# A mixture-of-experts stage: one-hot columns and places made an expert ahead, gathers and scatters at other experts

## The chip, the cores and the metric

The kernel runs on one core of a Trainium2 chip. The metric is device time in microseconds of one execution. TensorE multiplies matrices into PSUM banks, VectorE and ScalarE work on PSUM and SBUF, GpSimd on SBUF, and SyncE issues all transfers from HBM.

## The reference

Two layers over 256 latent tokens and 256 context tokens of width 1024. Each layer has four token mixers and then an expert-choice mixture of 16 experts, in which each expert takes the 32 tokens (CAP) with the highest affinity to it. In the last layer only the latent tokens go through the experts.

```python
def expert_choice_ffn(u, p):
    cap = max(1, EC_CAPACITY * n // N_EXPERTS)                  # 2 * 256 / 16 = 32
    aff = jax.nn.softmax((u @ p['w_router']).astype(jnp.float32), axis=-1)
    gate, idx = lax.top_k(jnp.swapaxes(aff, 1, 2), cap)
    xe = jax.vmap(lambda ub, ib: ub[ib])(u, idx)                # tokens of each expert
    hg, hu = jnp.split(jnp.einsum('becd,edf->becf', xe, p['w_exp_in']), 2, axis=-1)
    ye = jnp.einsum('becf,efd->becd', jax.nn.silu(hg) * hu, p['w_exp_out']) * gate[..., None].astype(u.dtype)
    return jax.vmap(lambda yb, ib: jnp.zeros((n, d), yb.dtype).at[ib.reshape(-1)].add(yb.reshape(-1, d)))(ye, idx)
```

## The kernel before

**Streams.** Layer 0 has two streams (context and latent tokens, ns = 2), the last layer one (ns = 1). An expert's 32 tokens of each stream stand side by side, so its products load 64 columns of tokens in layer 0 and 32 in layer 1, and the expert's weights stream past them.

**Order.** The program is written by generators, one for each part of the work. A planner (class Order) keeps modelled clocks of the engines, and each `yield` tells it a cost or a time to wait for; from that it fixes the order of the instructions at build time. On the chip each engine runs its own instructions in that order and waits on semaphores.

**Loads.** loader() writes the loads of each expert's weights: 8 of `w_ei` (rows of the first product) and 4 of `w_eo` (the second), 1 MB each, in the order first(1), second(0), first(2), second(1), and so on. A load goes into one of NB = 12 large buffers (L1701, L1707; the last expert's second weights L1704), or in four parts into tiles of the small pool t2 (L1699; NT2 = 40 tiles, which nearly all other short-lived tiles share). A load's buffer is free when TensorE has read it. The weights of layer 1's mixers (L888) come through the same queue and the same large buffers.

**Experts.** experts() runs over x = 0 to 15. first(x) (L1956, products L1964) makes the gate and up products; ScalarE and VectorE turn them into `a` (L1975 to L1977). second(x - 1) (L1980, products L1989) is written behind it, so that it covers the making of `a`; VectorE multiplies its rows by the modulation into `ye` (L2001, four instructions of 32x512 in layer 0). Then TensorE transposes `a` (L2026).

**Gathers.** Four experts (a group, eg = x // 4) are gathered at once by gather(eg) (L1827): VectorE spreads the chosen token numbers into `im` (L1831), TensorE broadcasts them over the partitions (L1837), VectorE compares them with each partition's number and scales them, which gives the one-hot columns `hot` (L1842), TensorE multiplies the tokens `h` by them (L1853), and ScalarE and VectorE write the result, modulated, to `xe` (L1860, L1862). Group 0 is gathered in choose(), at the end of the routing; groups 1, 2 and 3 behind the first product of experts 3, 4 and 5.

**Scatters.** columns() (L1814) makes, once, the table of token numbers and gates by column, behind the gather at expert 5. places(eg, s) (L1868, L1871) makes from it the one-hot places `ot` of a group for a stream; scatter() (L1874) multiplies `ye` by them (L1879) and VectorE adds the result to `h` (L1881). The groups 0, 1 and 2 are scattered at experts 6, 10 and 14, behind that expert's second(x - 1); group 3 in last_expert() (L1896, products L1924, scatter L1912, additions L1887), half by half, and behind it the next layer's norms and transposes begin. filters(1), layer 1's convolution filters, runs between the experts from expert 9 on.

Of the kernel before, what the change touches and what calls it, by code (L numbers as in the profile page):

```python
# [27 lines left out]
CAP = 32  # L28
# [185 lines left out]
def _a(n):  # L214
    return 0.19 + n / 1200


def _d(n):
    return 0.07 + n / 960
# [7 lines left out]
def kernel(ctx: ExitStack, tc: tile.TileContext, x, ctxt, cols, skip, lamb, fng, ta, tb, tcn, td,  # L227
# [169 lines left out]
    def layer(l):  # L397
        last = l == DEPTH - 1
        streams = (1,) if last else (0, 1)
        ns = len(streams)  # L400
# [1376 lines left out]
        def choose():  # L1777
# [23 lines left out]
            for r in range(CAP // 8):  # L1801
# [6 lines left out]
                e = yield {"pe": 0.3 if r == 0 else 0.0, "dve": 1.4}  # L1808
            nc.vector.tensor_copy(idxf, idxu)
            top["i"], top["v"] = idxf, vals  # L1810
            yield from gather(0)
            x_ev[1].t = S.t["pe"]

# [12 lines left out]

        def gather(eg):  # L1827

            n = 4 * CAP
# [9 lines left out]
            for i, s in enumerate(streams):  # L1839
                for b in range(2):  # L1840
                    t = 2 * s + b
                    nc.vector.tensor_scalar(hot[:, 2 * i + b], p[:, i * n:(i + 1) * n], iotac[:, b:b + 1],  # L1842
                                            r_tok[t], op0=OP.is_equal, op1=OP.mult)
            e = yield {"pe": 0.43, "dve": 2 * ns * _d(n)}
            yield e
            xe[eg] = [t2("xe", w=8 * M).rearrange("p (k e c) -> p k e c", k=2, e=4) for _ in range(KC // 2)]
# [102 lines left out]
        def experts():  # L1949


            yield rt_ev
            ye, eaT, pend = {}, {}, None
            mod5 = mods[l]["r5"][0]
# [25 lines left out]
            def second(x):  # L1980
# [22 lines left out]
                yield {"dve": _d(512) * 2 * ns}  # L2003

            for x in range(NE):
                a = yield from first(x)
                act = yield {"act": _a(FW), "dve": 2 * _d(FW)}
                if x == F1:
                    f_ev.t = act
                if x in (3, 4, 5):  # L2010
                    yield from gather(x - 2)
                if x == 5:
                    yield from columns()
                if x:
                    yield from second(x - 1)
                    if x % 4 == 0:
                        pend = x // 4 - 1
                if pend is not None and x % 4 >= 2:
                    y = ye.pop(pend)
                    for s in reversed(streams):  # L2020
                        yield from scatter(s, y[s], places(pend, s))
                    y = pend = None
                yield act
# [115 lines left out]
```

## Time and profile before

| | us |
|---|---|
| median of 3 runs | 2040.72 (2034.96 to 2045.57) |
| the profiled execution, its own time | 2040.19 |
| its span in the trace | 2038.3 |
| TensorE busy | 1706.0 (84%) |
| VectorE busy | 972.9 (48%) |
| ScalarE busy | 573.0 (28%) |
| layer 0's expert stage, about | 692 to 1190 |
| layer 1's expert stage, about | 1580 to 2020 |

The busy shares are means over stages that differ: in the mixers most of the work is on weights that are split on the chip, in the expert stages 192 loads of 1 MB pass in each layer. A busy TensorE is not TensorE at its peak, since its instructions overlap. The granted clock (PEclk) is given as a share of 2.4 GHz; 0.5 is 1.2 GHz.

### The profile page before, as it was taken

How to read it: one execution, taken by the hardware profiler on the slowest of the kernel's cores; microseconds unless marked ns; L12 is line 12 of the kernel's file. 1: busy time of each engine (PE TensorE's matmuls, PEld its weight loads, DVE VectorE, ACT ScalarE, POOL GpSimd, SP SyncE). 2: the span in 40 equal slices, each digit the busy share in tenths (PEclk: the TensorE clock that was granted, in tenths of full speed). 3: DMA queues.
4: the chain of work that ended last, by engine and by line, in shares of the span. 5: the costliest groups of instructions: out<-in, count | busy, mean ns of one | idle time of the engine just before them, and what ended most of it. 6: DMA issues, size and time to landing. Idle time of an engine off the chain costs nothing.

```text
span 2038.3 us, 28201 instructions
## 1 busy us (share of the span) xinstructions
PE 1706.0 (84%) x11128; PEld 1108.9 (54%) x11128; DVE 972.9 (48%) x1690; ACT 573.0 (28%) x1301; POOL 502.6 (25%) x413
## 2 busy tenths in 40 slices
PE   5878887899999899899799888988998877666655
PEld 2657565776789734533233268877997443222222
DVE  4788898966644412221232267778765111101012
ACT  4434555544432100100100054456552000000001
POOL 1466788612101100000000023786321000000000
PEclk9999898999999899999999999999998976767778
DMA  7535335232236699989999954555579999999997
GB/s 275 191 109 186 122 130 171 88 99 59 71 104 227 227 368 414 373 348 417 415 414 418 409 168 150 167 170 186 157 234 354 403 411 412 415 413 412 414 412 292
DMA packets 204973, 550.75 MB, mean 270 GB/s; under 512 B 14054, under 2 KB 94120, under 8 KB 174760
## 3 DMA queue, kind: packets, MB, share of 16 engines
q1 hardware_dynamic: 204840, 548.94, 71.5%
q8 instruction: 88, 1.44, 0.3%
q14 instruction: 45, 0.37, 0.1%
HBM read 547.83 MB, written 1.05 MB: 269 GB/s over the span
## 4 chain that ended last, share of the span: by engine, by line
PE 45%; DMA 28%; DVE 16%; ACT 5%; issue 3%; POOL 3%; SPq 0%; ACTq 0%; DVEq 0%; POOLq 0%
DMA we<-in_w_ei_dram 12%; PE pm L1964 9%; DMA we<-in_w_eo_dram 9%; PE pm L355 6%; PE pm L357 6%; PE pm L356 6%; PE psc L1989 5%; DVE wq L349 3%; DMA h<-in_w_ei_dram 3%; PE psc L1853 2%; ACT wq L348 2%; PE psc L1879 1%; DVE aj L526 1%; DMA wi<-in_w_in_dram 1%; DVE ca L1246 1%
## 5 line engine op out<-in xcount | busy, mean ns | idle before, releaser
L1964 PE MATMUL pm<-we,xe 128*32 128x256 f32 (+1 forms) x2848 | 383.2, 523 | 86.7 <-DMA we<-in_w_ei_dram 84.6
L355 PE MATMUL pm<-uh,wq 128*128 128x256 f32 (+1 forms) x832 | 293.1, 352 | 16.4 <-ACT tg L1001 8.0
L1964 PEld LDWEIGHTS pm<-we,xe 128*32 128x32 f32 (+1 forms) x2848 | 131.1, 132 | 315.4 <-issue 161.1
L356 PE MATMUL pm<-ul,wq 128*128 128x256 f32 (+1 forms) x832 | 284.0, 341 | 2.9 <-DVE ul L785 1.6
L357 PE MATMUL pm<-uh,wq 128*128 128x256 f32 (+1 forms) x832 | 283.4, 341 | 0.0
L349 DVE TENSOR_TENSOR wq<-wi,wq 128x1024 fp32r<-128x1024 f32 x131 | 181.7, 1398 | 112.5 <-ACT wq L348 112.3
L1989 PE MATMUL psc<-we,eaT 128*32 128x256 f32 (+1 forms) x1344 | 185.7, 530 | 46.4 <-DMA we<-in_w_eo_dram 45.0
L1976 DVE SCALAR_TENSOR_TENSOR ea<-ea,pm 128x512 f32<-128x512 f32 (+1 forms) x32 | 17.7, 555 | 392.2 <-ACT ea L1975 392.2
L528 POOL TENSOR_TENSOR aw<-aw,cb 128x512 f32<-128x512 f32 x124 | 193.1, 1571 | 14.9 <-DMA aw<-in_ada_t_dram 9.0
L355 PEld LDWEIGHTS pm<-uh,wq 128*128 128x128 f32 x832 | 162.3, 195 | 40.4 <-ACT tg L1001 8.9
L356 PEld LDWEIGHTS pm<-ul,wq 128*128 128x128 f32 x832 | 162.0, 195 | 21.8 <-issue 4.1
L357 PEld LDWEIGHTS pm<-uh,wq 128*128 128x128 f32 x832 | 161.5, 194 | 16.9
L2001 DVE TENSOR_TENSOR ye<-psc,modr 32x512 f32<-32x512 f32 (+1 forms) x120 | 66.4, 554 | 212.9 <-PE psc L1989 211.6
L1989 PEld LDWEIGHTS psc<-we,eaT 128*32 128x32 f32 (+1 forms) x1344 | 63.2, 134 | 161.9 <-issue 91.7
L348 ACT CAST wq<-wi 128x1024 fp32r<-128x1024 f32 x132 | 136.2, 1044 | 15.1 <-DMA wi<-in_w_in_dram 13.0
L1975 ACT ACTIVATE ea<-pm 128x512 f32<-128x512 f32 (+1 forms) x32 | 15.7, 490 | 425.3 <-PE pm L1964 396.2
L1246 DVE SCALAR_TENSOR_TENSOR ca<-up,colt,ca 128x510 f32<-128x510 f32 (+29 forms) x120 | 116.7, 973 | 2.3
L1893 POOL TENSOR_TENSOR hg<-h,gr 128x512 f32<-128x512 f32 x2 | 2.6, 1294 | 463.3 <-ACT px L360 459.4
L2028 ACT COPY eaT<-pt 128x512 f32<-128x512 f32 (+1 forms) x32 | 15.3, 479 | 319.2 <-PE pt L2026 319.2
L528 POOL TENSOR_TENSOR ao<-aw,cb 128x512 f32<-128x512 f32 x60 | 98.4, 1640 | 20.3 <-DMA aw<-in_ada_t_dram 17.7
L1292 ACT ACTIVATE e<-psc,nm 128x512 f32<-128x512 f32 (+1 forms) x72 | 44.3, 616 | 144.4 <-DVE nm L1290 144.0
L660 POOL MEMSET hf<- 1x256 f32 x4 | 1.5, 376 | 318.3 <-ACT ab L656 318.3
(408 smaller groups left out, 3002.4 us busy)
## 6 DMA issues: line engine op xcount, KB each, us to landing
we<-in_w_ei_dram SPq DMA_DIRECT2D x230, 1024.0 KB, 12.7
we<-in_w_eo_dram SPq DMA_DIRECT2D x113, 1024.0 KB, 14.6
wi<-in_w_in_dram SPq DMA_DIRECT2D x58, 1024.0 KB, 5.5
aw<-in_ada_t_dram SPq DMA_DIRECT2D x160, 256.0 KB, 5.6
h<-in_w_ei_dram SPq DMA_DIRECT2D x56, 256.0 KB, 14.5
we<-in_w_ei_dram SPq DMA_DIRECT2D x48, 256.0 KB, 7.4
wbr<-in_w_branch_dram SPq DMA_DIRECT2D x40, 256.0 KB, 5.3
we<-in_w_eo_dram SPq DMA_DIRECT2D x36, 256.0 KB, 5.9
```

What stands on the lines that cost most here:

```text
L348: nc.scalar.copy(hi, src)
L349: eng.tensor_tensor(lo, src, hi.bitcast(F32), op=OP.subtract)
L355: nc.tensor.matmul(out, lh, rh, start=first and i == 0, stop=False)
L356: nc.tensor.matmul(out, lh, rl, start=False, stop=False)
L357: nc.tensor.matmul(out, ll, rh, start=False, stop=last and i == n - 1)
L528: nc.gpsimd.tensor_tensor(o, wt_, cb[s, k], op=OP.mult)
L1246: nc.vector.scalar_tensor_tensor(o, up[:, :, max(d, 0):256 + min(d, 0)], cw[:, c0 + d:c0 + d + 1], o, op0=OP.mult, op1=OP.add)
L1292: nc.scalar.activation(e, p[:, :nk], AF.Exp, scale=scale, bias=nm, accum_out=s)
L1853: nc.tensor.matmul(p[:, kk * n:(kk + 1) * n], h[2 * s + b][k // 4][:, (k % 4) * 128:(k % 4 + 1) * 128], hot[:, 2 * i + b], start=b == 0, s ...
L1964: nc.tensor.matmul(dst[j * M:(j + 1) * M, :], lhs, w[o + j * FW // 512][:, j * FW % 512:j * FW % 512 + FW], start=k == 0, stop=k == KC - 1 ...
L1989: nc.tensor.matmul(py[j * M:(j + 1) * M, :FW], aT[:, c * 128 + q * M:c * 128 + (q + 1) * M], w[f % 2 * 2 + j * FW // 512][:, j * FW % 512: ...
L2001: nc.vector.tensor_tensor(ye[eg][s][c0 // 512][e4 * CAP:(e4 + 1) * CAP, c0 % 512:c0 % 512 + FW], py[r0:r0 + CAP, :FW], mod5[r0:r0 + CAP, c ...
```

## The change

gather() is cut in two: taken(eg) makes `im`, the broadcast and `hot`, and gather(eg) makes the products. For groups 1 to 3, taken() is written ahead of the first product of the expert behind whose first product gather() stands; group 0 keeps its order. The gathers are written at experts 3, 5 and 7 in place of 3, 4 and 5, the table of columns ahead of the first product of expert 6. The places are made behind the second product of experts 7, 9 and 12, and the scatters stand at experts 8, 10 and 13, between the first product of that expert and the second product of the one ahead, in place of 6, 10 and 14 behind the second product.

```diff
--- before.py
+++ after.py
@@ -1808,6 +1808,7 @@
                 e = yield {"pe": 0.3 if r == 0 else 0.0, "dve": 1.4}
             nc.vector.tensor_copy(idxf, idxu)
             top["i"], top["v"] = idxf, vals
+            yield from taken(0)
             yield from gather(0)
             x_ev[1].t = S.t["pe"]
 
@@ -1824,7 +1825,9 @@
                 nc.vector.tensor_scalar(ic[:, 8 * j:8 * j + 4 * ns], p[:, 8 * j:8 * j + 4 * ns], 0.5 if j else 1.0, None, op0=OP.mult)
             yield {"pe": 0.3, "dve": 0.6}
 
-        def gather(eg):
+        hots = {}
+
+        def taken(eg):
 
             n = 4 * CAP
             im = t2("im", w=ns * n)[:R]
@@ -1841,8 +1844,14 @@
                     t = 2 * s + b
                     nc.vector.tensor_scalar(hot[:, 2 * i + b], p[:, i * n:(i + 1) * n], iotac[:, b:b + 1],
                                             r_tok[t], op0=OP.is_equal, op1=OP.mult)
+            hots[eg] = hot
             e = yield {"pe": 0.43, "dve": 2 * ns * _d(n)}
-            yield e
+            if eg == 0:
+                yield e
+
+        def gather(eg):
+
+            n, hot = 4 * CAP, hots.pop(eg)
             xe[eg] = [t2("xe", w=8 * M).rearrange("p (k e c) -> p k e c", k=2, e=4) for _ in range(KC // 2)]
             for k4 in range(2):
                 for i, s in enumerate(streams):
@@ -1950,7 +1959,7 @@
 
 
             yield rt_ev
-            ye, eaT, pend = {}, {}, None
+            ye, eaT = {}, {}
             mod5 = mods[l]["r5"][0]
 
             def first(x):
@@ -2002,24 +2011,29 @@
                                                 py[r0:r0 + CAP, :FW], mod5[r0:r0 + CAP, c0:c0 + FW], op=OP.mult)
                 yield {"dve": _d(512) * 2 * ns}
 
+            ots, ready = {}, {3: 1, 5: 2, 7: 3}
             for x in range(NE):
+                if x in ready:
+                    yield from taken(ready[x])
+                if x == 6:
+                    yield from columns()
                 a = yield from first(x)
                 act = yield {"act": _a(FW), "dve": 2 * _d(FW)}
                 if x == F1:
                     f_ev.t = act
-                if x in (3, 4, 5):
-                    yield from gather(x - 2)
-                if x == 5:
-                    yield from columns()
+                if x in ready:
+                    yield from gather(ready[x])
+                if x in (8, 10, 13):
+                    pend = (8, 10, 13).index(x)
+                    y = ye.pop(pend)
+                    for s in reversed(streams):
+                        yield from scatter(s, y[s], ots.pop(s))
+                    y = None
                 if x:
                     yield from second(x - 1)
-                    if x % 4 == 0:
-                        pend = x // 4 - 1
-                if pend is not None and x % 4 >= 2:
-                    y = ye.pop(pend)
-                    for s in reversed(streams):
-                        yield from scatter(s, y[s], places(pend, s))
-                    y = pend = None
+                if x in (7, 9, 12):
+                    ots.update({s: places((7, 9, 12).index(x), s) for s in reversed(streams)})
+                    yield {"dve": ns * _d(256)}
                 yield act
                 p = pt()
                 for c in range(FW // 128):
```

## Rows read from the trace of the kernel before

**Rows 1.** The page: the span.

```profile
span 2038.3 us, 28201 instructions
```

**Rows 2.** Windows: length, busy time (count) by engine, PEclk, DMA share, GB/s.

```profile
692.00:1190.00 498.00, 446.18 (x2036) 177.68 (x2037) 130.62 (x258) 43.58 (x87) 7.60 (x11) 0.95 0.98 391
1200.00:1575.00 375.00, 336.05 (x2566) 310.72 (x2566) 274.29 (x460) 196.48 (x446) 179.23 (x154) 0.96 0.60 196
1580.00:2020.00 440.00, 303.91 (x3250) 133.77 (x3242) 56.59 (x135) 18.10 (x48) 0.00 (x0) 0.76 1.02 411
```

**Rows 3.** Windows inside layer 0's expert stage, same columns.

```profile
820.00:920.00 100.00, 89.88 (x430) 42.87 (x432) 27.37 (x57) 8.97 (x21) 0.00 (x0) 0.93 0.90 359
920.00:1170.00 250.00, 226.53 (x960) 76.84 (x958) 62.51 (x103) 17.27 (x28) 6.54 (x9) 0.97 1.02 415
860.00:870.00 10.00, 8.26 (x55) 6.24 (x55) 2.15 (x9) 3.01 (x8) 0.00 (x0) 0.84 0.40 167
900.00:910.00 10.00, 8.16 (x15) 3.35 (x16) 5.09 (x9) 0.00 (x0) 0.00 (x0) 0.83 1.01 410
```

**Rows 4.** Waits of SyncE's queue, 840 to 880: total us, times, longest.

```profile
SPq L1707 <- PE psc L1989: 21.3, 4, 17.5
```

**Rows 5.** Last expert's second weights, their source line; SyncE's timeline behind.

```profile
L1704 SPq DMA_DIRECT2D we<-in_w_eo_dram x4: 368/1813/4080, 1151.8 to 1159.4; - x4
DMA to landing us min/median/max: 14.4/14.9/15.9
...
1162.13 14.85 SPq L888 DMA_DIRECT2D wi<-in_w_in_dram  x4
```

**Rows 6.** Waits of TensorE, 740 to 1190: total us, times, longest.

```profile
PE psc L1879 <- DVE ot L1871: 13.4, 6, 3.4
PE pm L1964 <- DMA we<-in_w_ei_dram: 6.4, 9, 2.3
PE psc L1837 <- DVE im L1831: 5.2, 3, 1.8
PE psc L1989 <- DMA we<-in_w_eo_dram: 4.9, 8, 0.7
PE psc L1821 <- DVE vm L1819: 1.7, 1, 1.7
```

**Rows 7.** TensorE's timeline: start, length, instruction, [idle before it, releaser].

```profile
750.73 13.95 PE L1964 MATMUL pm<-we,xe 128*64 128x512 f32 x64
772.07 13.96 PE L1964 MATMUL pm<-we,xe 128*64 128x512 f32 x64
787.70 0.69 PE L1837 MATMUL psc<-im,ones 32*128 32x256 f32 x2 [1.68 <-DVE im L1831]
788.90 9.02 PE L1853 MATMUL psc<-hot,h 128*128 128x128 f32 x64 [0.51 <-DVE hot L1842]
839.02 13.95 PE L1964 MATMUL pm<-we,xe 128*64 128x512 f32 x64
```

**Rows 8.** VectorE's timeline around expert 3, same columns.

```profile
771.60 2.78 DVE L2001 TENSOR_TENSOR ye<-psc,modr 32x512 f32<-32x512 f32 x4 [5.62 <-PE psc L1989]
787.24 0.41 DVE L1831 TENSOR_TENSOR im<-idxf,tat 32x256 f32<-32x256 f32 x1
```

**Rows 9.** TensorE's timeline: first and last scatter of layer 0.

```profile
900.74 5.40 PE L1879 MATMUL psc<-ye,ot 128*128 128x512 f32 x8 [3.33 <-DVE ot L1871]
907.24 3.70 PE L1879 MATMUL psc<-ye,ot 128*128 128x512 f32 x8 [1.10 <-DVE ot L1871]
1138.10 6.56 PE L1879 MATMUL psc<-ye,ot 128*128 128x512 f32 x8 [3.32 <-DVE ot L1871]
```

**Rows 10.** TensorE's timeline: layer 0's last products, layer 1's first.

```profile
1171.95 3.67 PE L1924 MATMUL pm<-we,eaT 128*64 128x256 f32 x32 [0.72 <-ACT eaT L2028]
1178.51 3.67 PE L1924 MATMUL pm<-we,eaT 128*64 128x256 f32 x32
1192.80 0.35 PE L355 MATMUL pm<-uh,wq 128*128 128x256 f32 x1 [0.24 <-DVE uh L846]
```

## The prediction, made before the changed kernel had run

> **What bounds the kernel now.** I read the views from coarse to fine. First the span [rows 1] and the busy time of the stretches [rows 2]: layer 0's expert stage (692 to 1190 us) runs its transfers at a share of 0.98 of the DMA engines, layer 1's mixers (1200 to 1575) at 0.60, layer 1's expert stage (1580 to 2020) at 1.02. TensorE is busy for 446 of 498 us in the first and only 304 of 440 us in the last. So layer 1's experts are bound by weight transfers alone, and the moves there (gathers and scatters of one stream, half the columns) fall into time in which TensorE waits for weights anyway. The question is layer 0.
>
> There the stretches tell more [rows 3]. From 920 to 1170 us the transfers run at 415 GB/s with a share of 1.02: full. From 820 to 920 us they give 359 GB/s at a share of 0.90, and from 860 to 870 us only 167 GB/s at 0.40. In that hole nothing is left in the queue, because the queue of SyncE waits for TensorE to read a buffer free: one wait of 17.5 us for the second product (L1989) [rows 4]. The last transfers of the stage are issued up to 1159.4 us and land 14.4 to 15.9 us later [rows 5], at about 1174.5 us; TensorE comes to the last product only at 1178.51 and ends it at 1182.2 [rows 10]. So the stage is bound by transfers, with one hole in the middle, and with TensorE some 8 us late at the end.
>
> The hole's cause: an expert needs 12 loads of 1 MB (1.049 million bytes), at 415 GB/s 30.3 us of transfer, 2.53 a load. TensorE needs 21.3 us for an expert without extras (first products start at 750.73 and 772.07) [rows 7]. A gather adds 1.68 us of waiting, 0.69 for the broadcast product, 0.51 of waiting and 9.02 for the gather itself [rows 7], 11.9 us: 33.2 us, slower than the transfers. Experts 3, 4 and 5 have one each and expert 6 a scatter, so four in a row are slower than 30.3 us; the 12 large buffers (NB) fill with weights that TensorE has not reached, and the queue stops.
>
> **The change part by part, layer 0.** No instruction is added or taken away, no transfer is moved; im, the broadcast product and hot (L1831 to L1842), the column table (L1814) and the places (L1871) move on VectorE and TensorE, whole gathers and scatters move between experts.
>
> *Gathers at 3, 5, 7.* Experts now cost TensorE alternately about 33 and 21 to 25 us (expert 6 has the column table): at most 58 per pair against 60.6 us of transfer. Buffers are read faster than filled from expert 3 on. At expert 5 the first product now ends at 853.0 us (839.02 + 13.95 [rows 7]) and the queue runs dry about 11 us later (share 0.40 of the ten from 860 [rows 3]): it held 11 us of transfers. With the gather of expert 4 gone (11.9) and the broadcast in front of expert 3's and 5's first products (some 3.4 us of it at expert 5) this product ends at about 844.8, 8 us earlier; of the transfers some 2.5 us more have run, since the small hole ahead of 853 is gone too. The queue then holds 11 + 8 - 2.5, about 16 us, and the longest stretch without a release is the gather and the first load of the second product, 11 us. It does not run dry. The hole is worth 100 x (1 - 0.90/1.02) = 11.8 us by share and 100 x (1 - 359/415) = 13.5 us by bytes [rows 3]. I take 12.5 us off the end of the transfers; lower bound 10, if 2 us or so reappear at expert 3, where the broadcast now holds back the first release, upper bound 13.5.
>
> *im ahead of the first product.* What is queued behind the broadcast product is the whole first product. VectorE does im right behind the four products of the previous expert's rows, which begin as the second product ends and take 2.78 us [rows 8]; with im itself at 0.41 [rows 8] TensorE waits 3.2 us less the 0.5 in which it still transposes (771.60 to 772.07 [rows 7, 8]), about 2.7 us, in place of 1.68 + 0.51 = 2.2 us. The columns at expert 6 wait in the same way, 2.7 us in place of 1.7 [rows 6]. Together four waits of 2.7, 10.8 us, for 5.2 + 1.7 [rows 6] and three times 0.51 [rows 7], 8.4 us, now: 2.4 us worse on TensorE. That costs nothing on the end as long as TensorE is not the later one (sum below).
>
> *Scatters between a first and a second product.* Now the places and the rows' product stand between the second product and the scatter: waits of 13.4 us in six [rows 6], 3.33 + 1.10 in a pair [rows 9]. After the long wait the scatter's first half takes 5.40 and 6.56 us where the second half takes 3.70 [rows 9], and the granted clock of 900 to 910 us is 0.83 [rows 3], so part of it ran at 1.2 of 2.4 GHz: 1.7 and 2.9 us, with the third estimated like the smaller one 6.3 us. In the new place the expert's rows and the places are a whole expert old; the wait is nothing (upper bound: 1.10 each, if VectorE's additions hold back TensorE's banks). TensorE gains 13.4 + 6.3 = 19.7 us.
>
> *Where the gain goes.* From the first product at 772.07 to the last expert's at 1171.95 [rows 7, 10] TensorE now takes 399.9 us. Less 11.3 of waits for weights [rows 6], 19.7 of the scatters, plus 2.4: 370.9 us, so it could be at the last expert at 1143. The last expert's first load lands three loads (3 x 2.53 us) ahead of the last one: 1174.5 - 12.5 - 7.6 = 1154.4 us. So transfers set the end, with 11 us of slack on TensorE, and what the scatters save beyond that turns into waits for weights.
>
> *The end.* Now TensorE's last product ends 1182.2 - 1174.5 = 7.7 us after the last landing. If it waits for that load, what is left is half of this product, 1.85 us, and up to 2 us of the scatter between the halves: 2 to 4 us. Gain 5 us (4 to 6; none if TensorE stays late).
>
> *What follows.* Layer 1's first product comes 10.6 us after the end of the last product [rows 10], through norms and transposes of the same length; its first weights are issued at 1162.13, right behind the last expert's [rows 5], and move with them. Everything to the end then moves as a block: layer 1's transfers begin when its mixers allow.
>
> Sum: 12.5 + 5 = 17.5 us. The profiled execution took 2040.19 us (span 2038.3 [rows 1] and 1.9 around it), the median of the runs is 2040.72. 2040.2 - 17.5 = 2022.7: I say 2023 us.
>
> **A rule against the change.** The row first: after a wait of 3.33 us the scatter ran 1.7 us longer [rows 9], after 1.68 and 0.51 us the gather did not (9.02) [rows 7]. The new waits of 2.7 us lie between: at the price of the longer one each of the four costs 1.7 us more, 6.8 in all, and the slack of TensorE falls from 11 to about 4 us; at that of the shorter it stays 11. The sum is 17.5 either way. The Trainium skill, "TensorE: Matmul & The Clock Gate", section "Why this matters for your kernels", says that idle gaps between bursts of products put TensorE back to half its clock, so that the products behind the gap pay too; by this rule it would be the longer one's price, and rival 1 would gain. No row here shows a gap of just this length.
>
> **The rivals.**
> 1. *TensorE becomes the late one.* The four new waits, slower products behind them and the filters of layer 1 (from expert 9 on) eat the slack of 4 to 11 us and some 8 more. The transfers still lose their hole, but TensorE's tail or a new hole hands it back. For it: experts 3, 5 and 7 are near 33 us and expert 8 has a scatter at once. Against it: TensorE is freed of 19.7 us. It gives a gain of 2 to 9 us: 2031 to 2038, middle 2035. Chance 0.20.
> 2. *Slower: SyncE's queue blocks on a small buffer.* hot now lives through a first product, the places through one more expert, ye[0] until expert 8. They share the 40 small buffers with those loads that are split in four. SyncE issues in order; a split load whose buffer was a scatter's blocks all behind it. One such stop is priced in the trace: a wait of 17.5 us left at least 6 us of dead queue (share 0.40 in ten) and at most the whole hole of 12.5 [rows 3, 4]; I take 9. It decides from the fourth such stop (17.5 - 4 x 9 = -18): 2059; three give 2050. Against it: gathers at 3, 5, 7 hold 8 tiles of xe at once in place of 12. Chance 0.08.
> 3. *The written order of layer 1 shifts.* The order is planned with modelled clocks that this change moves; in layer 1's mixers TensorE is busy for 336 of 375 us [rows 2], so 39 us of idle time can grow or shrink. A fifth of it, some 8 us, comes on top either way: 2015 or 2031, no gain if half as much idle time is added, and slower than the bound below from 28 us. Chance 0.10.
>
> **How the numbers follow.** The forecast has 0.62, its own range 2018 to 2027 (gains of 10 + 3 to 13.5 + 8). Over 0.5% (10.2 us, about what three runs of this kernel can tell, 2034.96 to 2045.57) faster: 0.62, 0.04 of rival 1, 0.04 of rival 3: 0.70. Within 0.5%: 0.16 of rival 1, 0.03 of rival 3: 0.19. Slower: 0.08 and 0.03: 0.11. The range takes in rival 1 and the near side of rival 3: 2014 to 2038.
>
> **What the changed profile would show.** Right: transfers at over 405 GB/s in every 10 us from 740 to about 1160 us; no wait of SyncE for L1989 over 10 us; no wait of L1879 for ot; L1837 behind im for about 2.7 us at experts 3, 5 and 7; waits for weights in experts 14 and 15; the last product of layer 0's latent rows ending near 1164 us; layer 1's stretches as long as now. Wrong: a new hole near experts 7 and 8, TensorE with no waits for weights at experts 14 and 15, waits of SyncE on scatters, or a mixer stage of another length.

## The result, and the profile after

The changed kernel takes 2027.92 us, the median of ten runs (2021.55 to 2031.09), beside 2042.76 us for ten runs of the kernel before (2034.96 to 2048.35). The ratio is 0.9931, interval 0.9913 to 0.9948: 14.1 us faster (10.6 to 17.8). The forecast was 17.5 us. The profiled execution took 2030.58 us, its span is 2028.8.

**The hole is gone.** The windows that answer to [rows 3], with two of ten that the new waits fall into:

```profile
820.00:920.00 100.00, 91.63 (x433) 36.72 (x430) 21.28 (x44) 7.16 (x15) 0.00 (x0) 0.91 1.02 418
920.00:1160.00 240.00, 225.84 (x987) 80.01 (x986) 70.14 (x118) 19.70 (x35) 6.93 (x9) 0.99 1.02 416
840.00:850.00 10.00, 10.00 (x38) 3.04 (x36) 0.80 (x3) 0.00 (x0) 0.00 (x0) 0.77 1.02 406
900.00:910.00 10.00, 10.00 (x34) 3.17 (x36) 1.37 (x4) 0.00 (x0) 0.00 (x0) 0.70 1.02 409
```

From 820 to 920 us the transfers now give 418 GB/s in place of 359, at a share of 1.02 in place of 0.90. The share is the busy share of the DMA engines. In both tens it is 1.02, while the granted clock falls to 0.77 and 0.70. So TensorE was slower there and the transfers did not notice.

SyncE's queue no longer stops for long. Its wait for the second product, 700 to 1180 us (total, times, longest):

```profile
SPq L1707 <- PE psc L1998: 62.2, 27, 8.8
```

The longest is 8.8 us, in place of 17.5 [rows 4], and nothing shows that it costs time: from 820 to 1160 us the share stays at 1.02, so the queue still holds transfers.

TensorE's waits from 740 to 1180 us, as [rows 6]:

```profile
PE psc L1840 <- DVE im L1834: 8.4, 3, 2.8
PE pm L1973 <- DMA we<-in_w_ei_dram: 5.5, 10, 0.8
PE psc L1998 <- DMA we<-in_w_eo_dram: 5.0, 8, 0.7
PE psc L1822 <- DVE vm L1820: 2.7, 1, 2.7
PE psc L1888 <- DVE h L1890: 1.9, 1, 1.9
```

The 13.4 us behind the places are gone. The broadcasts wait 8.4 us in three, the columns 2.7. The waits for weights (L1973 and L1998) sum to 10.5 us; 9.7 of them lie behind 1080 us, in the last experts. One wait of 1.9 us stands ahead of a scatter, for VectorE's addition to `h`.

TensorE's timeline: two of the new waits with what follows them, a scatter, and the end of the stage, as [rows 7, 9, 10]:

```profile
782.79 0.95 PE L1840 MATMUL psc<-im,ones 32*128 32x256 f32 x2 [2.75 <-DVE im L1834]
783.67 15.34 PE L1973 MATMUL pm<-we,xe 128*64 128x512 f32 x64
798.95 7.49 PE L1862 MATMUL psc<-hot,h 128*128 128x128 f32 x64
...
839.33 16.52 PE L1973 MATMUL pm<-we,xe 128*64 128x512 f32 x64
...
899.94 1.19 PE L1840 MATMUL psc<-im,ones 32*128 32x256 f32 x2 [2.82 <-DVE im L1834]
901.06 16.38 PE L1973 MATMUL pm<-we,xe 128*64 128x512 f32 x64
917.37 7.41 PE L1862 MATMUL psc<-hot,h 128*128 128x128 f32 x64
...
946.20 7.13 PE L1888 MATMUL psc<-ye,ot 128*128 128x512 f32 x16
...
1006.92 4.56 PE L1888 MATMUL psc<-ye,ot 128*128 128x512 f32 x10 [1.92 <-DVE h L1890]
...
1161.00 1.94 PE L1998 MATMUL psc<-we,eaT 128*64 128x512 f32 x8 [0.63 <-DMA we<-in_w_eo_dram]
1164.53 3.85 PE L1933 MATMUL pm<-we,eaT 128*64 128x256 f32 x32 [1.00 <-ACT eaT L2042]
1171.26 3.67 PE L1933 MATMUL pm<-we,eaT 128*64 128x256 f32 x32
...
1185.53 0.35 PE L355 MATMUL pm<-uh,wq 128*128 128x256 f32 x1 [1.88 <-ACT u L838]
```

Two of the three scatters are one piece of 7.13 us for both streams, with no wait ahead; the middle one has the wait of 1.92 us inside it. The first products behind the new waits take 15.34, 16.52 and 16.38 us where the kernel before needs 13.95 [rows 7], and the gathers shown behind them 7.49 and 7.41 in place of 9.02. At the end the second products wait for a load (0.63), so TensorE has caught up. The last product ends at 1171.26 + 3.67 = 1174.9 us, and layer 1's first product comes 10.6 us later, as before [rows 10].

The last expert's second weights, issue and landing, as [rows 5]:

```profile
L1704 SPq DMA_DIRECT2D we<-in_w_eo_dram x4: 2620/4484/4767, 1143.3 to 1157.3; - x4
DMA to landing us min/median/max: 14.6/16.6/18.7
```

The last of the four is issued at 1157.3; with the shortest landing, 14.6 us, it is there at 1171.9. TensorE ends 3.0 us behind it. In the kernel before, the last one is issued at 1159.4 and has the shortest landing too, 14.4 [rows 5]: it is there at 1173.8, and TensorE ends 8.4 us behind it.

**Stages, not spans.** In the traces the stage does not begin at the same time, although TensorE's instructions ahead of it are the same: its first broadcast product comes between 700 and 710 us. So each stage is measured from its own start. "Stage" is from layer 0's first broadcast product to the end of the last product of the latent rows; 10.6 us of norms follow; "mixers" is from layer 1's first product to layer 1's first broadcast product; "rest" is from there to the end. The last column is what the transfers moved from 820 to 930 us.

| kernel | stage begins | stage | mixers | rest | GB/s |
|---|---|---|---|---|---|
| before | 700.6 | 481.6 | 381.2 | 464.2 | 365 |
| before, a second execution | 703.4 | 479.6 | 381.3 | 466.3 | 377 |
| after | 708.6 | 466.4 | 380.2 | 463.0 | 418 |
| gathers, first scatter at 8 | 710.4 | 465.9 | 381.0 | 463.5 | 418 |
| scatters alone | 704.6 | 472.9 | 384.0 | 464.5 | 395 |
| one-hot columns behind | 709.9 | 463.6 | 380.8 | 462.2 | 418 |
| no scatters | 700.3 | 464.1 | 378.9 | 463.8 | 417 |
| layer 1 alone | 708.7 | 479.2 | 380.5 | 464.0 | 369 |
| scatters twice | 703.4 | 469.2 | 381.8 | 463.9 | 416 |
| last scatter at 14 | 703.1 | 465.7 | 381.6 | 463.5 | 417 |
| more room, before | 701.2 | 481.9 | 380.9 | 466.4 | 370 |
| more room, columns behind | 701.4 | 468.0 | 382.0 | 463.7 | 410 |
| more room for longer, before | 700.6 | 478.1 | 384.0 | 464.5 | 383 |
| columns behind, scatter at 14 | 703.5 | 464.9 | 384.8 | 464.8 | 417 |

Three executions in which layer 0 is as before (481.6, 479.6, 479.2) have a mean of 480.1 us; after has 466.4: 13.7 us less, close to the 14.1 of the runs. Mixers (380.2) and rest (463.0) lie within 1 us of the nearest of these three (380.5 and 464.0). One trace tells such a stretch to a few us only: over all fourteen, mixers go from 378.9 to 384.8 and rest from 462.2 to 466.4.

### The profile page after: what moved, and what is told of

It reads as the page before. It is cut to its first block, busy times and chain, and to the rows that moved or that the text cites. A ratio compares the mean times of both kernels' runs of the same rounds, so it can differ in the third digit from the quotient of the medians.

```text
span 2028.8 us, 28213 instructions
## 1 busy us (share of the span) xinstructions
PE 1713.3 (84%) x11128; PEld 1109.7 (55%) x11128; DVE 973.3 (48%) x1690; ACT 573.0 (28%) x1301; POOL 503.6 (25%) x413
## 4 chain that ended last, share of the span: by engine, by line
PE 46%; DMA 28%; DVE 15%; ACT 4%; issue 3%; POOL 3%; SPq 0%; ACTq 0%; DVEq 0%; POOLq 0%
PE pm L1973 10%; DMA we<-in_w_eo_dram 10%; DMA we<-in_w_ei_dram 9%; PE pm L355 6%; PE pm L357 6%; PE pm L356 6%; PE psc L1998 4%; DMA h<-in_w_ei_dram 3%; DMA h<-in_w_eo_dram 3%; DVE wq L349 3%; PE psc L1862 2%; DVE aj L526 1%; DVE aw L526 1%; ACT wq L348 1%; POOL aw L528 1%
## 5 line engine op out<-in xcount | busy, mean ns | idle before, releaser
L1973 PE MATMUL pm<-we,xe 128*32 128x256 f32 (+1 forms) x2912 | 407.1, 543 | 97.9 <-DMA we<-in_w_ei_dram 96.0
L1973 PEld LDWEIGHTS pm<-we,xe 128*32 128x32 f32 (+1 forms) x2912 | 136.0, 136 | 345.2 <-issue 186.9
L1998 PE MATMUL psc<-we,eaT 128*32 128x256 f32 (+1 forms) x1280 | 171.6, 510 | 35.0 <-DMA we<-in_w_eo_dram 33.5
L348 ACT CAST wq<-wi 128x1024 fp32r<-128x1024 f32 x132 | 136.2, 1044 | 15.2 <-DMA wi<-in_w_in_dram 13.0
L1998 PEld LDWEIGHTS psc<-we,eaT 128*32 128x32 f32 (+1 forms) x1280 | 58.7, 129 | 143.8 <-issue 74.3
## 6 DMA issues: line engine op xcount, KB each, us to landing
we<-in_w_eo_dram SPq DMA_DIRECT2D x110, 1024.0 KB, 14.6
```

The source lines that it names most:

```text
L348: nc.scalar.copy(hi, src)
L1973: nc.tensor.matmul(dst[j * M:(j + 1) * M, :], lhs, w[o + j * FW // 512][:, j * FW % 512:j * FW % 512 + FW], start=k == 0, stop=k == KC - 1 ...
L1998: nc.tensor.matmul(py[j * M:(j + 1) * M, :FW], aT[:, c * 128 + q * M:c * 128 + (q + 1) * M], w[f % 2 * 2 + j * FW // 512][:, j * FW % 512: ...
```

## The experiments

My theory: the result is the hole of the transfers, which the gathers at 3, 5, 7 close, plus the tail; the columns ahead and the scatters between the products are worth little or nothing by themselves. The rivals: it comes from the 19.7 us that the scatters free on TensorE; it comes from layer 1; and, for the columns, that their new waits cost something on the end.

**1. The gathers, in the old form of everything else** (`e1_gathers_only`): the kernel before, with the gathers at 3, 5, 7 and, since group 3 is there later, the table behind the gather at 7 and the first scatter at 8, which has to follow the last gather; one-hot columns, places and scatters in the old form. So it is not the gathers alone that move: the first scatter leaves expert 6 here too.

```diff
-                if x in (3, 4, 5):
-                    yield from gather(x - 2)
-                if x == 5:
+                if x in (3, 5, 7):
+                    yield from gather((x - 1) // 2)
+                if x == 7:
                     yield from columns()
...
-                if pend is not None and x % 4 >= 2:
+                if pend is not None and x in (8, 10, 14):
```

> The kernel before with its gathers at experts 3, 5 and 7 in their old form, the table of columns behind the gather at 7, and group 0 scattered at 8 in the old form (it has to stand behind the last gather, which reads the same h); the scatters of groups 1 and 2 stay at 10 and 14, behind the second product, with their places made just ahead. Theory (the gain is the hole in the transfers): the hole of 820 to 920 us is gone, transfers end some 12 us earlier; the last scatter still stands in the tail with its wait and slow half, so TensorE is late by 6 us or so: 8 to 12 us faster than the kernel before. Rival (the gain is TensorE's waits ahead of the scatters): all six waits are still there, so 0 to 2 us.

Measured: 2029.76 us, ratio 0.9943 (0.9921 to 0.9965), 11.6 us faster. TensorE's waits, 740 to 1190 us:

```profile
PE psc L1879 <- DVE ot L1871: 13.4, 6, 3.4
PE psc L1989 <- DMA we<-in_w_eo_dram: 2.5, 4, 0.7
PE pm L1964 <- DMA we<-in_w_ei_dram: 1.1, 2, 0.6
```

The waits for the places are all there (13.4 us), TensorE waits for weights only 3.6 us, and still the transfers run at 418 GB/s through the place of the hole. The last load lands at about 1170.8 us and the last product ends at 1176.3, 5.6 us later, against 3.0 after. So the gathers at 3, 5, 7 with the first scatter at 8 close the hole, without columns ahead or scatters in the new place, and bring about four fifths of the result by the medians (11.6 of 14.1, with intervals that overlap).

**2. The scatters alone** (`e2_scatters_only`): the changed kernel with gathers, one-hot columns and table where they were before.

```diff
...
-            ots, ready = {}, {3: 1, 5: 2, 7: 3}
+            ots, ready = {}, {3: 1, 4: 2, 5: 3}
...
-                if x in ready:
-                    yield from taken(ready[x])
-                if x == 6:
-                    yield from columns()
...
                 if x in ready:
+                    yield from taken(ready[x])
                     yield from gather(ready[x])
+                if x == 5:
+                    yield from columns()
```

> The changed kernel with its gathers and columns where and as they were before (behind the first products of 3, 4 and 5); the places ahead and the scatters at 8, 10 and 13 between a first and a second product are kept. Theory: the hole at experts 4 and 5 stays, some 11 of 12.5 us of it, and only the tail gains: 3 to 7 us faster than the kernel before. Rival (TensorE's waits): 13 us of waits and 6 us of slow products are gone, so nearly the whole gain, 12 to 18 us.

Measured: 2033.5 us, ratio 0.9981 (0.9964 to 0.9998), 3.9 us faster (0.4 to 7.3). Windows of this kernel:

```profile
820.00:930.00 110.00, 102.68 (x528) 45.09 (x526) 26.68 (x56) 10.76 (x24) 0.00 (x0) 0.98 0.97 395
910.00:920.00 10.00, 10.00 (x48) 3.16 (x44) 1.37 (x2) 0.60 (x1) 0.00 (x0) 1.00 1.03 420
930.00:1160.00 230.00, 205.69 (x866) 67.92 (x862) 64.55 (x105) 16.09 (x26) 6.92 (x9) 1.00 1.02 416
```

and of the second execution of the kernel before (`before_again`, nothing edited, one execution of 2043.15 us):

> The kernel before once more, for a second profile. Every profile so far reaches layer 0's first broadcast product at another time (700 to 710 us) with the same instructions ahead of it. Expected if that is scatter between executions: again some time between 698 and 712 us; the stage from that product to the end of the last expert's last product 478 to 484 us, with a hole of 10 to 13 us in the transfers at experts 4 to 6; if the hole depends much on the execution, 5 to 13 us and a stage of 474 to 484.

```profile
820.00:930.00 110.00, 99.27 (x490) 44.84 (x486) 29.45 (x60) 10.16 (x23) 0.00 (x0) 0.97 0.93 377
910.00:920.00 10.00, 10.00 (x47) 3.64 (x47) 1.62 (x3) 0.58 (x1) 0.00 (x0) 1.00 0.86 333
930.00:1160.00 230.00, 206.63 (x864) 70.90 (x862) 59.76 (x99) 16.08 (x26) 6.54 (x9) 0.96 1.02 416
```

Against 416 GB/s the kernel before loses 110 x (1 - 377/416) = 10.3 us in the first window, which lies in the 10 to 13 expected (as its stage of 479.6 us does in 478 to 484); this one loses 5.6. I had expected nearly the whole hole to stay. The scatter that has left expert 6 accounts for a part: from 910 to 920 us, right behind where that scatter stands in the kernel before (901.0 to 911.2 us in `before_again`), 420 GB/s pass in place of 333, which is 10 x (420 - 333)/416 = 2.1 of the 4.7 us. The other 2.6 lie ahead of it, above all from 830 to 840 us (417 in place of 328 GB/s), where TensorE's order is that of the kernel before; they can be a difference between two executions. The two parts, 11.6 and 3.9 us, sum to 15.5, which the whole's 14.1 (10.6 to 17.8) covers; but both have the first scatter at expert 8, so this is no clean split into gathers and scatters.

**3. One-hot columns behind the first product** (`e3_columns_behind`): the changed kernel, with taken() right ahead of gather().

```diff
...
-                if x in ready:
-                    yield from taken(ready[x])
                 if x == 6:
                     yield from columns()
...
                 if x in ready:
+                    yield from taken(ready[x])
                     yield from gather(ready[x])
```

> The changed kernel with the one-hot columns made behind the first product, right ahead of the gather, as before; all else as changed. Theory: TensorE has slack to the end, so the columns made ahead are worth nothing: the changed kernel's time within 2 us (13 to 17 us faster than the kernel before). Rival (the waits count): the changed form has 2.7 us waits in place of 2.2 and slower first products, so this one would be 3 to 6 us faster than the changed kernel.

Measured: 2025.6 us, ratio 0.9925 (0.9903 to 0.9948), not to be told from the changed kernel. That part of the change is worth nothing that these runs can measure. Two of its gathers in TensorE's timeline, and the windows that they lie in:

```profile
853.05 9.02 PE L1861 MATMUL psc<-hot,h 128*128 128x128 f32 x64 [0.51 <-DVE hot L1845]
912.76 7.51 PE L1861 MATMUL psc<-hot,h 128*128 128x128 f32 x64 [0.50 <-DVE hot L1845]
```

```profile
850.00:860.00 10.00, 7.82 (x51) 7.24 (x50) 4.43 (x11) 1.46 (x4) 0.00 (x0) 0.83 1.02 425
910.00:920.00 10.00, 7.93 (x66) 7.51 (x66) 4.13 (x11) 2.99 (x8) 0.00 (x0) 1.00 1.03 425
```

The same wait of 0.50 us, behind 1.67 us for the broadcast, stands ahead of both. Where the granted clock of the ten is 0.83 the gather takes 9.02 us, where it is 1.00 it takes 7.51.

**4. No scatters** (`e4_no_scatters`): the changed kernel without the scatters of groups 0 to 2 in layer 0, so its output lacks what these experts add there.

```diff
-                        yield from scatter(s, y[s], ots.pop(s))
+                        if last:
+                            yield from scatter(s, y[s], ots.pop(s))
+                        ots.pop(s, None)
```

> The changed kernel without the scatters of groups 0 to 2 in layer 0 (their rows are not added to h, places are still made). 21.4 us of TensorE's work and 24 additions on VectorE are gone. Theory: transfers set the end of the stage: the changed kernel's time within 2 us. Rival (TensorE sets the end): 15 to 21 us faster than the changed kernel.

Measured: 2026.15 us, ratio 0.9931 (0.9906 to 0.9957): three times 7.13, 21.4 us of work, are gone from TensorE, and nothing is gained that can be measured. Its waits for weights:

```profile
PE pm L1973 <- DMA we<-in_w_ei_dram: 16.7, 27, 2.3
PE psc L1998 <- DMA we<-in_w_eo_dram: 8.2, 14, 0.8
```

They are 24.9 us, in place of 10.5: 14.4 of the 21.4 us are seen to turn into waits for weights. So TensorE does not set the end of the stage.

**5. Layer 1 alone** (`e5_layer1_only`): layer 0 in the order of before, layer 1 in that of after.

```diff
...
+            ots, ready = {}, {3: 1, 5: 2, 7: 3} if last else {3: 1, 4: 2, 5: 3}
+            sc = (8, 10, 13) if last else (6, 10, 14)
             for x in range(NE):
+                if x in ready and last:
+                    yield from taken(ready[x])
...
+                if x in ready:
+                    if not last:
+                        yield from taken(ready[x])
+                    yield from gather(ready[x])
...
```

> The change made in layer 1 alone; layer 0 written as before. Theory (layer 1 is bound by weights, share 1.02, and TensorE waits there anyway): the kernel before within 3 us, and the stretch from layer 1's first broadcast product to the end within 2 us of 464. Rival (the waits taken away in layer 1 count): some 5 us faster.

Measured: 2038.2 us, ratio 0.9989 (0.9972 to 1.0006); "rest" is 464.0 us, before 464.2 and 466.3. Layer 1 gains nothing that can be measured.

**6. The scatters twice** (`e6_scatters_twice`): the changed kernel, each scatter product of layer 0 written twice.

```diff
-                    nc.tensor.matmul(p, ot[:, b * 128:(b + 1) * 128], ye[n], start=True, stop=True)
+                    for _ in range(1 if last else 2):
+                        nc.tensor.matmul(p, ot[:, b * 128:(b + 1) * 128], ye[n], start=True, stop=True)
```

> The changed kernel with each product of the scatters of groups 0 to 2 in layer 0 made twice into the same bank: 21.4 us more of TensorE's work. Theory (transfers set the end, TensorE has slack): what TensorE waits for weights in the changed kernel, 10 us, is eaten first, and the rest counts: 5 to 12 us slower than the changed kernel. Rival (TensorE sets the end): some 21 us slower than the changed kernel, slower than the kernel before.

Measured: 2030.68 us, ratio 0.9958 (0.9937 to 0.998), by the medians of the ratios some 5.5 us slower than the changed kernel; the intervals still overlap. TensorE now waits for weights nowhere from 740 to 1190 us. Two windows show small holes, at a clock of 1.00, and TensorE's timeline has a doubled scatter ahead of each:

```profile
950.00:960.00 10.00, 10.00 (x40) 3.33 (x38) 1.82 (x3) 0.00 (x0) 0.00 (x0) 1.00 0.84 314
1110.00:1120.00 10.00, 10.00 (x47) 3.33 (x47) 2.60 (x5) 0.58 (x1) 0.00 (x0) 1.00 0.84 310
```

```profile
939.15 14.00 PE L1889 MATMUL psc<-ye,ot 128*128 128x512 f32 x32
...
1097.08 14.00 PE L1889 MATMUL psc<-ye,ot 128*128 128x512 f32 x32
```

SyncE's timeline around the first (start, length, x issues):

```profile
930.68 8.91 SPq L1701 DMA_DIRECT2D we<-in_w_ei_dram  x6
955.06 3.80 SPq L1707 DMA_DIRECT2D we<-in_w_eo_dram  x3
```

The scatter holds TensorE for 14.00 us, to 953.15, in which it reads no weights and frees no buffer; SyncE issues nothing from 939.6 to 955.06. Each hole costs 10 x (1 - 312/416) = 2.5 us, the two together 5. So 21.4 us more on TensorE cost at most a part of themselves: 5.5 us by the medians, not clear of the noise, and 2.8 us by the two stages (469.2 and 466.4). What they cost is hardly at the end (the last product ends 3.7 us after the last landing) but in new holes. The doubled scatter between these two, at 1001.99 us, opens none.

**7. The last scatter at expert 14** (`e7_last_scatter_14`), as in the kernel before, but in the new form, between a first and a second product:

```diff
-                if x in (8, 10, 13):
+                if x in (8, 10, 14):
...
-                if x in (7, 9, 12):
+                if x in (7, 9, 13):
```

> The changed kernel with the scatter of group 2 at expert 14 in place of 13, its places at 13; all else as changed. It stands one expert nearer to the end, without the wait for the places. Theory (its 7 us fall into waits for weights at experts 14 and 15): the changed kernel's time within 2 us. Rival (the place alone makes the gain at the end): the 4 us of the tail are lost, 3 to 5 us slower than the changed kernel.

Measured: 2026.35 us, ratio 0.9923 (0.9896 to 0.9951). Whether expert 13 or 14 has it makes no difference that can be measured.

**8 to 10. More room for the loads.** If the hole is only that 12 large buffers are full, more room should close it without a move. `e8_more_buffers_before` is the kernel before with two loads of each of the experts 3 to 6 of layer 0 in the small pool, in four parts; `e10_more_buffers_long` does so up to expert 9, and `e9_more_buffers_e3` does that in the kernel of experiment 3.

```diff
-                    elif large():
+                    elif large() and not (l == 0 and 3 <= e <= 6 and i in (3, 7)):
```

> The kernel before, with two of the eight first-product loads of experts 3 to 6 of layer 0 put into small tiles (four parts each) in place of large buffers, so that some two more loads fit ahead of TensorE; the order of all work is that of before. Theory (the queue stops because the 12 large buffers are full): some 2 x 2.53 us of the hole at experts 4 to 6 are gone, 3 to 7 us faster than the kernel before. Rival (the order of gathers and scatters on TensorE is what counts): within 2 us of the kernel before, and the hole as large.

> e3_columns_behind with the same two loads of experts 3 to 9 of layer 0 in small tiles. Theory: with gathers at 3, 5 and 7 the buffers are never full, so more of them are worth nothing: within 2 us of e3_columns_behind (13 to 17 us faster than the kernel before). Rival (transfers still lack buffers somewhere): 2 to 5 us faster than e3_columns_behind.

> e8_more_buffers_before with the two loads in small tiles up to expert 9 in place of 6. In e8 the transfers lost nothing from 830 to 850 us any more, but more from 900 to 920, where the loads go back to the 12 large buffers while TensorE is still behind. Theory (full buffers stop the queue, and the room must last until TensorE has caught up): no loss over 0.1 of a 10 us stretch after 890 us and a mean over 820 to 930 us above 385 GB/s (before: 359 over 820 to 920); in time 0 to 5 us faster than the kernel before, since loads in four parts run somewhat slower (411 against 416 GB/s in e9). Rival (the order on TensorE sets the loss, whatever the room): mean over 820 to 930 us at 360 to 375 GB/s, and no faster.

Measured: e8 2042.34 us, ratio 0.9999 (0.9977 to 1.0021); e9 2031.15, 0.9951 (0.9934 to 0.9968); e10 2039.41, 0.9995 (0.9972 to 1.0019). The windows around the hole, of the kernel before,

```profile
830.00:850.00 20.00, 20.00 (x102) 7.71 (x102) 4.12 (x8) 1.82 (x5) 0.00 (x0) 1.00 0.89 348
860.00:880.00 20.00, 18.26 (x99) 9.58 (x99) 4.89 (x13) 3.60 (x9) 0.00 (x0) 0.90 0.60 221
900.00:920.00 20.00, 18.16 (x62) 6.96 (x64) 6.46 (x11) 0.58 (x1) 0.00 (x0) 0.91 0.98 381
```

of e8,

```profile
830.00:850.00 20.00, 20.00 (x105) 8.16 (x105) 4.12 (x8) 2.29 (x6) 0.00 (x0) 1.00 1.03 410
860.00:880.00 20.00, 18.26 (x101) 10.07 (x102) 5.80 (x16) 3.59 (x9) 0.00 (x0) 0.88 0.84 327
900.00:920.00 20.00, 17.40 (x58) 6.73 (x60) 7.22 (x12) 0.58 (x1) 0.00 (x0) 0.91 0.69 259
```

and of e10, the last two:

```profile
860.00:880.00 20.00, 18.26 (x99) 9.55 (x100) 5.06 (x14) 3.60 (x9) 0.00 (x0) 0.91 0.79 304
900.00:920.00 20.00, 18.22 (x62) 7.01 (x64) 6.41 (x11) 0.59 (x1) 0.00 (x0) 0.91 0.98 378
```

With e8 the transfers are full from 830 to 850 us (410 in place of 348 GB/s), lose less from 860 to 880 (327, before 221), and lose more from 900 to 920 (259, before 381). A part of the hole has moved, behind the experts that have the room, for TensorE is no less behind there. With the room up to expert 9 that later loss is no larger than in the kernel before (378, 381), and the mean of 820 to 930 rises to 383 GB/s (365, 377 and 369 in three executions with layer 0 as before), just short of the 385 that I expected; the hole of 860 to 880 stays in part (304). The time is not to be told from that of the kernel before; a gain of up to 5.7 us lies inside the interval. A part of the gain can be lost again on the loads in four parts, as e9 shows, where there is no hole to close: 780 to 950 us of e9 and, below it, of the kernel of experiment 3,

```profile
780.00:950.00 170.00, 160.59 (x796) 71.23 (x794) 43.70 (x88) 16.14 (x36) 0.00 (x0) 0.97 1.03 411
```

```profile
780.00:950.00 170.00, 160.75 (x798) 71.08 (x796) 44.85 (x89) 16.14 (x36) 0.00 (x0) 0.97 1.02 416
```

With the loads in four parts the transfers go at 411 in place of 416 GB/s, which is 2 us of these 170. By the medians of the ratios e9 is some 5 us slower than experiment 3 (stage 468.0, not 463.6), but the two intervals overlap. My expectations of a gain of 3 to 7 us in e8 and of no loss over 2 us in e9 failed by the medians; e10's 0 to 5 us held (1.0). That the split loads eat up e10's gain fits these numbers but was not measured apart.

**11. Both harmless parts together** (`e11_e3_e7`): experiment 3 with the last scatter at expert 14.

```diff
...
                 if x in ready:
+                    yield from taken(ready[x])
                     yield from gather(ready[x])
-                if x in (8, 10, 13):
...
+                if x in (8, 10, 14):
...
```

> The two variants that were nominally fastest together: one-hot columns made behind the first product, and the last scatter at expert 14. Theory (transfers set the end): the changed kernel within 2 us, so no better (12 to 17 us faster than the kernel before). Rival (both gain): 3 to 6 us faster than the changed kernel.

Measured: 2026.21 us, ratio 0.9926 (0.9902 to 0.9951). No run gave a version that can be told from the changed kernel on the better side.

## Why the prediction came true, point by point

**The bound and the hole.** That layer 0's experts are bound by transfers, with a hole that TensorE's reading causes, is shown: without the scatters nothing is gained (4), and with the gathers spread and the first scatter behind them the hole closes (1). Its price was sized at 12.5 us. From the start of the stage to the last landing it takes 1173.8 - 700.6 = 473.2 us before and 1171.9 - 708.6 = 463.3 after, 9.9 us less, just under the lower bound of 10. (The prediction had the last landing before at 1174.5; the trace has 1173.8.) In the two other executions with layer 0 as before the same stretch is 471.2 and 473.7 us; against the mean of the three it is 9.4 us less. Through the hole itself after gains more, but it has lost some 2 us ahead of it: from 728 to 768 us it moves 300 and 377 GB/s, where the kernel before moves 325 and 401 in the same stretch of its stage, 8 us earlier: 20 x (25 + 24)/415 = 2.4 us. There TensorE's instructions are the same, and why the rate differs stays open. In the second execution of before the hole is 10.3 us, in that of experiment 5 110 x (1 - 369/416) = 12.4: one execution gives this term to 2 or 3 us only.

One step of the reasoning was too strict: each pair of experts was to take TensorE at most 58 us, against 60.6 of transfer. From first product to first product, experts 3 and 4 take 55.7 us after (783.67 to 839.33), but 5 and 6 take 61.7 (to 901.06), since their first products run slower, and in experiment 1 experts 7 and 8 take 70.4 (891.49 to 961.87). No hole opens in either place. The running sum fits the traces better: experts 3 to 6 take 117.4 us after and 139.2 before (772.07 to 911.31), against 4 x 30.3 = 121.2 of transfer.

**The columns ahead.** The waits came as worked out: 2.75, 2.83 and 2.82 us at the broadcasts and 2.7 at the columns, for 2.7 each. What I read wrongly stands in the rule against the change: that after 1.68 and 0.51 us "the gather did not" run longer. It did. 9.02 us was a gather at a lower granted clock; at 1.00 it takes 7.41 to 7.51 (3). So the shorter wait already has a price, about 1.6 us, and the longer one takes 1.4, 2.6, 1.7 and 2.4 us from the first products (15.34, 16.52, 15.65, 16.38 against 13.95), 8.1 us in four. That is the dearer of the two cases, 6.8 us, and more; the gathers give back some 4.8 of it, three times 1.6. In the tens of these products the granted clock is 0.70 to 0.83. The Trainium skill, "TensorE: Matmul & The Clock Gate", section "Why this matters for your kernels", says of longer idle gaps between bursts than these that they put TensorE back to half its clock; by that row alone these waits need not have cost anything, so here the measured clock decides, and my use of the row for gaps of 2.7 us went further than the row. On the end it all costs nothing that can be measured, as forecast: experiment 3, without the waits at the broadcasts, is no slower and no faster.

**The scatters.** All six waits of 13.4 us are gone; forecast was no wait, measured one of 1.9 us in all. The work of the three scatters falls from 28.3 to 21.7 us, 6.6 less where 6.3 was estimated, so TensorE gains 18.1 us of the 19.7. That what TensorE gains beyond the transfers turns into waits for weights is seen in the last experts (9.7 us) and more than doubled in experiment 4. That there is slack is borne out by both sides: 21.4 us less gain nothing that can be measured, 21.4 us more cost some 5.5 by the medians. Taken at face value that is nearer 16 us than the 4 to 11 that I named, but the 5.5 are not clear of the noise. And the slack is not one sum at the end: more work in one piece can open a hole where it stands, as two of the three doubled scatters did (6). (The sum behind the 11 us has a slip: 399.9 less 11.3 and 19.7, plus 2.4, is 371.3 and not 370.9. The 1143 and the 11 us stand.)

**The tail.** Forecast 2 to 4 us behind the last landing in place of 7.7, a gain of 5; measured 3.0 in place of 8.4, a gain of 5.3. The kernels with the last scatter in the new form, or with none, end 3.0 to 3.2 us behind the landing (after, 2, 3, 4, 7, 11), and 3.7 with it doubled (6). Those with the old form end 5.6 to 8.4 us behind it: before 8.4 in both executions, experiment 5, with layer 0 as before, 5.6, and experiment 1 also 5.6. So the scatters count here, for 2.5 to 5.3 us. That this is the step from the 11.6 of experiment 1 to the 14.1 of the whole is not shown: the intervals overlap, and the profiled stage of experiment 1 (465.9) is no longer than that of after (466.4), since its last load lands some 3 us sooner from the stage's start.

**The sum and the time.** 9.9 + 5.3 = 15.2 us is what the two profiled stages differ by (481.6 - 466.4); 14.1 is what the runs show, and 17.5 was forecast. The mis-sized term is the hole, 2.6 to 3.1 us of it; the tail came about as sized. The 2027.92 us lie in the wide range of 2014 to 2038 and 0.9 us above the forecast's own of 2018 to 2027, which also counts the tail with 3 to 8 us where its paragraph has 4 to 6. The gain of 14.1 lies inside 13 to 21.5, near its lower end. I had named an end near 1164 us for the last product and full transfers from 740; it ended at 1174.9, 8 us of it because the stage began that much later than in the trace of before. The transfers are full from 770 to 1160, with a 400 and a 402 among the tens. Such positions are those of one execution and tell little of the change.

**The rivals.** TensorE does not become the late one (3, 4). SyncE does not block on a small buffer: its longest wait for the second product is 8.8 us, the one for a small tile's load (L1699) 3.6, for another load and not for TensorE. Layer 1's order costs nothing that can be measured: mixers 380.2 us (before 381.2, 381.3), and layer 1's part alone is worth nothing that can be measured (5).

**Open.** Why the stage begins between 700 and 710 us and loses a different amount at its start; why the part of experiment 2's hole that lies ahead of the scatter is smaller too; how the gain divides between the spread gathers and the first scatter's move to 8, since no run has the gathers at 3, 5, 7 with that scatter still at 6; and whether more room, without split loads, would do as well as moving the gathers: that was not tried.

## What to carry to other kernels

Where transfers set the end, look not at the mean but at tens of microseconds: a hole in the transfers with full buffers behind it is the place to gain. Here it closed when the extra work was spread so that a run of four steps took less than its transfers (117.4 us against 121.2), though one pair in it took more. Work taken from the other engine beyond that turned into waits for data (21.4 us less, nothing gained), and more buffers for four steps moved part of the hole to where they end. Measure stages from their own start, and before calling a duration undisturbed look at the granted clock over it.

## What the runs showed that I had not expected

- Behind waits of TensorE as short as 1.68 and 0.51 us the clock was lower in most cases, but not in all: the same gather took 9.02 us in a ten with a granted clock of 0.83 and 7.51 us in one with 1.00, behind the same waits (experiment 3). Over the ten traces with the gathers in the old form, 25 of 30 took 8.97 to 9.21 us and five took 7.51.
- With identical instructions ahead, layer 0's expert stage began anywhere from 700.3 to 710.4 us in fourteen traces, a spread of 10 us beside the 14 that the change is worth. Even with the stage measured from its own start, three traces with layer 0 written as before differ by up to 2.4 us.
- With some 1 MB loads in four parts the transfers moved 411 GB/s where whole ones moved 416, with no hole in either. The kernel with more of them (experiment 9) was about 5 us slower by the medians, with intervals that overlap.
